# The short convolution's projections: two outputs by seven block products on x scaled by r, and the second projection in one piece in a written-out order

## The chip, the cores and the metric

The kernel runs on one core of one Trainium2 chip. The metric is the device time of one execution in microseconds; the time of a kernel is the median over its runs. All data are fp32.

## The reference

The kernel computes a trunk of two layers on 1024 tokens of width 1024. Every sub-layer works on a normed input and adds its result to x. The first layer's token mixer is a gated short convolution, and it is the part that is changed:

```
h = rmsnorm(x) * gain            # x (1, 1024, 1024)
b, c, xv = split(h @ w_in, 3)    # w_in (1024, 3072)
u = b * xv
y = causal depthwise convolution of u, width 3
x = x + (c * y) @ w_out          # w_out (1024, 1024)
x = x + swiglu(rmsnorm(x))       # hidden width 2816
```

The second layer has attention in a window of 128 in place of the convolution, and a SwiGLU of its own.

## The kernel before

**Products.** Activations lie transposed, with channels on partitions and the 1024 tokens along the free axis, as eight tiles X0 to X7. TensorE multiplies fp32 data as a rounded part hi (fp32r) and the rest lo; a product is hi*hi + hi*lo + lo*hi. `product_step` (L155, L159) does this for one block of 128 input channels: six matmuls of 128x512, three for each half of the tokens. One output tile of 128 channels takes eight steps, 48 matmuls, in two PSUM banks. Weights come by SP's queue into WR; `Weights.split` makes hi (WH, L127, or L129 on DVE) and lo (WL, L130) on the engines that it is given: in the first loop ACT and POOL, later ACT and DVE.

**Norm.** The projection multiplies x times gain, without r, the token's 1/rms. `finish_x` (L197 to L208) makes hi and lo of x times gain in XS0 to XS7 and adds up the squares. `token_r_rows` (L238) then gets r, the same on all partitions, with four 128x512 matmuls by a matrix of ones (L250, L251) in P2 and P3. As r was left out, the outputs b and xv are multiplied by its row afterwards (`times`, L173), and y once more for c.

**The projection's order.** `conv_layer` first goes over the eight input blocks as x lands, with three output tiles at once: b0, x0 and c0. Then for j = 1 to 7 it does the tiles b_j, x_j and c_j. In between, DVE and ACT make u = b*x, the taps of the convolution (L358, L360), y*r (L363), and z_j = c*y as hi and lo. After x_1 and c_1, all eight output tiles of w_out get the part of z0 and z1 (`w_out_part`), 12 matmuls for each half; the part of z2 to z7 comes at the beginning of `channel_mixer`, 18 for each half. The order of this stage is what the program order and the free buffers make it. In four of the eight turns DVE also makes sums of the mixer's first weights (`weight_sums`, L436 to L439), placed behind a given operation, which go to HBM as `first_sums`.

**The written-out order.** `channel_mixer` has an order of its own, the class `Line`. `work` appends matmuls at the line's end, at `MM` = 0.2265 us for each; `at(t, f)` puts any other step at the line time t; `run` then issues all steps so that whatever is due goes ahead of the matmuls that begin later. The line times are a plan; on the chip the engines run by their queues and semaphores. A weight's split is due `LEAD` = 13 us ahead of its first matmul and its load 7 us ahead of that.

**Seven block products.** In the mixer two output tiles of 128 channels are computed together as a 2x2 block product over pairs of input blocks and the two halves of the tokens, with seven block products for eight (the scheme of Strassen in Winograd's form). A block product (`unit_product`, `ring_granule`, `granule_work`, L544 to L547) is 12 matmuls of 128x512 on operands B[0] to B[6], which are sums and differences of blocks of x, and on weights of which four of seven are sums. The first four pairs (GROUP) run kind by kind, with sums that lie in HBM; the later ones are steady, pair by pair, with sums that DVE makes beside them. `put` makes hi (L475, ACT) and lo (L476, DVE) of an operand, and the split of a granule does the same for weights, in eight slots named G. The results are combined in `sa` and `s3`.

**The end of the convolution.** `tail_item` (L622 to L641) does one output tile of the second projection for one half of the tokens, adds it to X, and squares it; `half_chain` (L670 to L682) then makes r for that half by four 128x1 matmuls and four transposes, which leave the rows of r in a PSUM bank, and L692 scales x by the gain and those rows in place.

Of the kernel before, what the change touches and what calls it, by code (L numbers as in the profile page):

```python
# [3 lines left out]

# [5 lines left out]
F32 = mybir.dt.float32  # L10
# [4 lines left out]
P = 128  # L15
# [53 lines left out]
SUMS = {2: 0, 3: 1, 5: 2, 6: 3}  # L69
# [11 lines left out]
def trunk_kernel(ctx: ExitStack, tc: tile.TileContext, xT, small, w_in, w_out, w_qk, w_v, w_o, w_gu, w_dn, out):  # L81
# [21 lines left out]
    class Weights:  # L103
# [84 lines left out]
    def finish_x(stage, m, first, hi_eng=act, ss_eng=pool, parts=1):  # L188
# [13 lines left out]
        if first:  # L202
            state["ss"] = slot("G1")
            act.activation(state["ss"], X[m], AF.Square)
        else:
            sq = slot(("G2", "G9")[m % 2])
            act.activation(sq, X[m], AF.Square)
            ss_eng.tensor_tensor(state["ss"], state["ss"], sq, ALU.add)  # L208
# [67 lines left out]
    def conv_layer():  # L276
        groups = [[0, 1], [2, 3, 4, 5, 6, 7]]
        z = {}

        def w_out_part(g, m):  # L280
            js = groups[g]
            run(residual_tile(w_out[m][:, js[0] : js[-1] + 1, :], [z[j] for j in js], m))

        def in_tile(m, tags=("acc", "acc")):
            ps = Acc(tags)
            run(product(ps, load_w(w_in[m], NK), xs))
            return ps
# [3 lines left out]
        wb, wx, wc = Weights(), Weights(), Weights(("G6", "G7", "G8"))  # L291

        def load_b(k, n):
            wb.load(w_in[0][:, k : k + n, :], k, n)

        def load_parts(k, n):
            load_b(k, n)
            wx.load(w_in[2 * NK][:, k : k + n, :], k, n)
            wc.load(w_in[NK][:, k : k + n, :], k, n)
# [15 lines left out]
        wx.load(w_in[2 * NK][:, 0:1, :], 0, 1)  # L315
        wc.load(w_in[NK][:, 0:1, :], 0, 1)
        load_x(1)
        load_parts(1, 1)
        for k in range(NK):
# [12 lines left out]
            run(product_step(ps_b, wb, state["xs"][k], k, k == 0, k == NK - 1))  # L332
            run(product_step(ps_x, wx, state["xs"][k], k, k == 0, k == NK - 1))
            run(product_step(ps_c, wc, state["xs"][k], k, k == 0, k == NK - 1))
        xs = [state["xs"][k] for k in range(NK)]
        b0 = slot("G10")
        for src, c in ps_b.parts:
            act.copy(b0[:, c], src)
        rb = token_r_rows()

        for j in range(NK):
            t1 = slot(f"G{3 + j % 2}")
            if j > 0:
                ps_b = in_tile(j)
                times(t1, ps_b, rb)
            else:
                dve.tensor_tensor(t1, b0, rb, ALU.mult)
            if j == 2:
                for m in range(NK):
                    w_out_part(0, m)  # L350
            if j > 0:
                ps_x = in_tile(2 * NK + j)
            u = slot(f"G{5 + j % 2}")
            times(u, ps_x, rb)
            dve.tensor_tensor(u, u, t1, ALU.mult)
            y = slot(f"G{7 + j % 2}")
            cw = [cst[:, C_CONV + w * NK + j : C_CONV + w * NK + j + 1] for w in range(NCONV)]
            act.activation(y, u, AF.Copy, scale=cw[2])  # L358
            for s in (1, 2):
                dve.scalar_tensor_tensor(  # L360
                    y[:, s:T], u[:, 0 : T - s], cw[2 - s], y[:, s:T], ALU.mult, ALU.add
                )
            y_op = dve.tensor_tensor(y, y, rb, ALU.mult)  # L363
            if j > 0:
                ps_c = in_tile(NK + j)
            if 3 <= j < 7:
                n = j - 3
                for i in (0, 1):
                    weight_sums(first_sums[0][n], w_gu[0, n], w_gu[0, NF + n], 2 * i, 2, f"G{9 + i}", "G11", behind=y_op)
            z[j] = pair_slot(f"A{j % 6}")  # L370
            for c in [slice(0, T)] if j + 1 < NK else [lo_half, hi_half]:
                for src, cc in ps_c.parts:
                    if c.start <= cc.start < c.stop:
                        dve.tensor_tensor(y[:, cc], src, y[:, cc], ALU.mult)
                act.copy(z[j][:, 0, c], y[:, c])
                dve.tensor_tensor(z[j][:, 1, c], y[:, c], plain(z[j][:, 0, c]), ALU.subtract)
        js = groups[1]
# [64 lines left out]
    def weight_sums(dst, w1, w2, j0, n, raw_tag, sum_tag, line=None, t=0.0, behind=None):  # L442
# [10 lines left out]
        def add():  # L453
            raw = it["raw"]
            s = it["s"] = slot(sum_tag, (P, 4, 2 * P), bufs=2 if sum_tag == "WL" else 1)[:, :, 0 : n * P]
            for f in sums_of(raw[:, 0, 0], raw[:, 0, 1], raw[:, 1, 0], raw[:, 1, 1], s[:, 0], s[:, 1], s[:, 2], s[:, 3]):
                op = f()
                if behind is not None:
                    issue_behind(op, behind, "of use to the mixer only")
# [13 lines left out]
    def split_steps(out_hi, out_lo, raw):  # L473
# [1254 lines left out]
```

## Time and profile before

| | |
|---|---|
| median of 3 runs | 1975.11 us (1974.98 to 1975.17) |
| profiled execution | 1974.93 us |
| its span | 1973.1 us |
| PE, matmuls | 99% of the span busy |
| PEld, weight loads | 83% |
| DVE / ACT / POOL | 67% / 41% / 14% |
| TensorE clock granted | 1.0 of full speed |
| transfers | 293.96 MB, mean 149 GB/s |

Times are microseconds unless marked ns. PE is TensorE's matmuls and PEld its weight loads, which overlap them; DVE is VectorE, ACT ScalarE, POOL GpSimd, SP SyncE, whose queue issues most loads. A line of the order of time has the start, the duration, the engine, the source line, the operation, output<-inputs by the program's names, partitions x elements, and a count; in brackets stands the idle time before it and who ended it. A line of the waits has who waited for whom, the total, the number of times and the longest. A line of the windows has the length, then busy time and instructions of PE, PEld, DVE, ACT and POOL, the granted clock, the DMA engines' busy share and GB/s. A line of the transfers has output<-input, the issuing queue, the count, the size of one and its median time to landing.

### The profile page before, as it was taken

To read this page: it belongs to the slowest core of one execution; us is meant where nothing else is said; L and a number is where in the kernel's file an instruction comes from. 1 tells how busy PE (TensorE), PEld (TensorE's weight loads), DVE (VectorE), ACT (ScalarE), POOL (GpSimd) and SP (SyncE) were. 2 spreads that over 40 slices of the span, in tenths; PEclk is the share of its full clock that TensorE was granted. 3 is DMA by queue.
4 is the path that set the end of the run, shared out by engine and by line. 5 is a ranking of instruction groups with operands and counts; after the bars stand their busy time and mean duration, and the time that the engine had idled before them with its cause. 6 is when DMAs were issued, how large, how long until landed. Compare 5 with 4: busy or idle time off the path is not lost.

```text
span 1973.1 us, 25617 instructions
## 1 busy us (share of the span) xinstructions
PE 1963.0 (99%) x9253; PEld 1637.8 (83%) x9253; DVE 1323.0 (67%) x2367; ACT 808.6 (41%) x1557; POOL 270.9 (14%) x399
## 2 busy tenths in 40 slices
PE   9999999999999999999999999999999999999999
PEld 7888888888888888888898888888888888888887
DVE  7545457767767667765745888888677777675543
ACT  5111125533333334444524777645333333344441
POOL 4000001001111111000003445410011111110000
PEclk9999999999999999999999999999999999999999
DMA  5123325245555546986410000051455554478563
GB/s 176 33 75 113 111 92 186 77 148 186 188 174 184 190 149 238 336 289 204 130 52 22 22 7 17 28 185 58 158 176 182 197 190 164 148 264 278 202 225 104
DMA packets 139214, 293.96 MB, mean 149 GB/s; under 512 B 13520, under 2 KB 56528, under 8 KB 139088
## 3 DMA queue, kind: packets, MB, share of 16 engines
q1 hardware_dynamic: 116064, 212.08, 32.2%
q0 software_dynamic: 22880, 80.23, 11.1%
q8 instruction: 73, 1.20, 0.2%
q14 instruction: 53, 0.43, 0.1%
q10 hardware_dynamic: 144, 0.03, 0.0%
HBM read 207.87 MB, written 84.41 MB: 148 GB/s over the span
## 4 chain that ended last, share of the span: by engine, by line
PE 95%; DVE 3%; ACT 1%; DMA 1%; issue 1%; ACTq 0%; DVEq 0%
PE acc L155 14%; PE acc L544 13%; PE acc L547 13%; PE acc L545 13%; PE P L547 8%; PE P L544 8%; PE P L545 8%; PE acc L159 7%; PE acc L624 1%; PE acc L622 1%; PE acc L623 1%; PE P L1363 1%; PE P L1311 1%; PE P L1100 1%; PE P L1188 1%; PE P L1312 1%
## 5 line engine op out<-in xcount | busy, mean ns | idle before, releaser
L155 PE MATMUL acc<-XS,WH 128*128 128x512 f32 x1152 | 325.5, 395 | 0.8 <-ACT WH L127 0.6
L544 PE MATMUL acc<-XS,G 128*128 128x512 f32 x774 | 301.6, 390 | 0.0
L547 PE MATMUL acc<-XS,G 128*128 128x512 f32 x774 | 301.2, 389 | 0.0
L545 PE MATMUL acc<-XS,G 128*128 128x512 f32 x774 | 301.1, 389 | 0.0
L155 PEld LDWEIGHTS acc<-XS,WH 128*128 128x128 f32 x1152 | 207.6, 188 | 37.2 <-ACT WH L127 0.7
L159 PE MATMUL acc<-XS,WL 128*128 128x512 f32 x576 | 178.2, 391 | 0.0
L547 PEld LDWEIGHTS acc<-XS,G 128*128 128x128 f32 x774 | 145.3, 188 | 30.2
L545 PEld LDWEIGHTS acc<-XS,G 128*128 128x128 f32 x774 | 145.3, 188 | 30.1
L544 PEld LDWEIGHTS acc<-XS,G 128*128 128x128 f32 x774 | 145.3, 188 | 30.0
L544 PE MATMUL P<-A,G 128*128 128x512 f32 x422 | 164.2, 389 | 0.0
L545 PE MATMUL P<-A,G 128*128 128x512 f32 x422 | 164.2, 389 | 0.0
L547 PE MATMUL P<-A,G 128*128 128x512 f32 x422 | 164.2, 389 | 0.0
L547 PE MATMUL acc<-A,G 128*128 128x512 f32 x370 | 143.9, 389 | 0.0
L544 PE MATMUL acc<-A,G 128*128 128x512 f32 x370 | 143.9, 389 | 0.0
L545 PE MATMUL acc<-A,G 128*128 128x512 f32 x370 | 143.9, 389 | 0.0
L475 ACT CAST G<-WR 128x512 fp32r<-128x512 f32 (+1 forms) x172 | 103.6, 603 | 63.2 <-PE acc L547 31.1
L476 DVE TENSOR_TENSOR G<-WL,G 128x512 fp32r<-128x512 f32 x144 | 98.6, 686 | 45.7 <-ACT G L475 45.7
L791 ACT ACTIVATE G<-G 128x512 f32<-128x512 f32 x88 | 55.7, 633 | 161.9 <-DVE G L862 157.8
L476 DVE TENSOR_TENSOR G<-WR,G 128x512 fp32r<-128x512 f32 (+1 forms) x172 | 114.3, 665 | 10.7 <-ACT G L475 10.4
L127 ACT CAST WH<-WR 128x256 fp32r<-128x256 f32 (+2 forms) x81 | 46.5, 583 | 178.7 <-PE acc L155 154.7
L159 PEld LDWEIGHTS acc<-XS,WL 128*128 128x128 f32 x576 | 104.2, 188 | 18.1
L475 ACT CAST G<-WH 128x512 fp32r<-128x512 f32 (+1 forms) x136 | 81.4, 599 | 75.4 <-PE acc L547 39.5
(301 smaller groups left out, 3883.6 us busy)
## 6 DMA issues: line engine op xcount, KB each, us to landing
G<-h SPq DMA_DIRECT2D x70, 512.0 KB, 5.0
h<-X POOLq DMA_DIRECT2D x44, 512.0 KB, 5.2
X<-in_w_dn SPq DMA_DIRECT2D x80, 256.0 KB, 3.7
s<-X POOLq DMA_DIRECT2D x40, 512.0 KB, 4.8
WR<-in_w_gu SPq DMA_DIRECT2D x36, 512.0 KB, 6.2
WH<-in_w_gu SPq DMA_DIRECT2D x36, 512.0 KB, 6.7
h<-X POOLq DMA_DIRECT2D x66, 256.0 KB, 3.9
WR<-s SPq DMA_DIRECT2D x44, 256.0 KB, 3.5
```

The lines of the kernel that those rows point to most:

```text
L127: act.copy(self.hi[:, c], self.raw[:, c])
L155: pe.matmul(ps.half(h), wh, xs[:, j, c], start=first and j == 0, stop=False)
L159: pe.matmul(ps.half(h), wl, xs[:, 0, c], start=False, stop=last)
L475: lambda: act.copy(out_hi, raw),
L476: lambda: dve.tensor_tensor(out_lo, raw, plain(out_hi), ALU.subtract),
L544: pe.matmul(ps, w[:, 0, c], x[:, 0, :], start=start and e == 0, stop=False, skip_group_check=True)
L545: pe.matmul(ps, w[:, 0, c], x[:, 1, :], start=False, stop=False, skip_group_check=True)
L547: pe.matmul(ps, w[:, 1, c], x[:, 0, :], start=False, stop=last, skip_group_check=True)
L622: pe.matmul(ps, hi[:, kc], xs[:, 0, c], start=k == 0, stop=False)
L623: pe.matmul(ps, hi[:, kc], xs[:, 1, c], start=False, stop=False)
L624: pe.matmul(ps, lo[:, kc], xs[:, 0, c], start=False, stop=k == n_op - 1)
L791: state["silu"] = act.activation(x, x, AF.Silu)
```

## The change

- The rows of r are made before the projection ends, from `mean` (eight 128x1 matmuls) and `turn` (eight transposes), and stay in P2 and P3. X is scaled by gain and r in place (`scale`).
- The tiles b0, x0 and c0 are computed as before in the first loop, and c1 behind them, all from x without r. They go to HBM (`keep`), come back later (`back`) and are then multiplied by r's rows.
- The other 20 output tiles are ten pairs (`plan_`): b_j with x_j for j = 1 to 7, and c2 with c3, c4 with c5, c6 with c7. Each is done by seven block products on the scaled X. Four pairs form the group, whose weight sums POOL makes at the start, in place and by way of HBM (`sums_in_place`); six are steady.
- The last two block products of the last pair are interleaved with the first half of the first two tiles of the second projection (`lead_in`), which now takes all eight z at once, 24 matmuls for each half of a tile.
- The whole stage has the written-out order of a `Line`, which the mixer continues.
- The mixer's own first sums are made by POOL, in place, in eight pieces during the steady pairs; the lo parts of the first weights are made by DVE and no longer by POOL.
- w_in lies in HBM as pairs of blocks (`_pair_tiles`), so that the loads of the first tiles are runs of 128 floats (`load_pairs`).

`scheme` and `operands_of` are the functions of the mixer's order and its `put`, moved out so that both stages can use them.

```diff
-SUMS = {2: 0, 3: 1, 5: 2, 6: 3}
+SUMS = {2: 3, 3: 0, 5: 2, 6: 1}
...
+        def load_pairs(self, src, k0, n):
+            c = slice(k0 * P, (k0 + n) * P)
+            p = slice(k0 // 2 * P, (k0 + n + 1) // 2 * P)
+            nc.sync.dma_start(
+                self.raw[:, c].rearrange("p (k e c) -> p e k c", e=min(n, 2), c=P),
+                src[:, k0 % 2 if n == 1 else 0 : k0 % 2 + 1 if n == 1 else 2, p].rearrange("p e (k c) -> p e k c", c=P),
...
-        groups = [[0, 1], [2, 3, 4, 5, 6, 7]]
...
+        xs = {}
...
-        wb, wx, wc = Weights(), Weights(), Weights(("G6", "G7", "G8"))
+        wb, wx, wc = Weights(), Weights(), Weights(("G8", "G6", "G7"))
+        wc1 = Weights(("G9", "G10", "G8"))
...
-                wb.split(k, n, act, pool)
-                wx.split(k, n, act, pool)
-                wc.split(k, n, act, pool)
+                for w in (wb, wx, wc):
+                    w.split(k, n, act, dve)
...
+            if k < NK - 2:
+                for ps, w in ((ps_b, wb), (ps_x, wx), (ps_c, wc)):
+                    run(product_step(ps, w, state["xs"][k], k, k == 0, False))
...
-        rb = token_r_rows()
-        for j in range(NK):
...
+            wc1.split(k, 2, act, dve)
...
+        line = Line()
+        at = line.at
+        line.end = -2 * 18 * MM
+        for k in (NK - 2, NK - 1):
+            for ps, w in ((ps_b, wb), (ps_x, wx), (ps_c, wc)):
+                line.work(6, run, product_step(ps, w, xs[k], k, False, k == NK - 1))
...
+        def mean():
+            ps = bank("P3")
+            for b in range(NB):
+                pe.matmul(ps[:, b : b + 1], state["ss"][:, b * P : (b + 1) * P], ones, start=True, stop=True)
+            r["m"] = slot("rs_m", (P, NB))
+            r["r"] = slot("r", (P, NB))
+            dve.tensor_scalar(r["m"], ps[:, 0:NB], 1.0 / D, EPS, ALU.mult, ALU.add)
+            rsqrt(r["r"], r["m"], (P, NB))
+        def turn():
+            for h in (0, 1):
+                rows[h] = bank(("P2", "P3")[h])
+                for b in range(4):
+                    row = r["r"][:, 4 * h + b : 4 * h + b + 1]
+                    pe.transpose(rows[h][:, b * P : (b + 1) * P], row.to_broadcast([P, P]), ident)
+        at(-7.6, mean)
+        at(-5.0, turn)
+        tools = scheme(line, ["G0", "G3", "G6", "G7", "G1", "G2", "G4", "G5"])
...
+        plan_ = [("bx", 1), ("bx", 2), ("bx", 3), ("cc", 2), ("bx", 4), ("bx", 5), ("cc", 4), ("bx", 6), ("bx", 7), ("cc", 6)]
...
+        in_sums = [tc.dram_tile((4, P, 4 * P), F32, name=f"s0_{u}") for u in range(GROUP)]
+        for u in range(GROUP):
+            sums_in_place(line, in_sums[u], *sources(u), 0, 4, f"A{2 + u}", -30.0 + u, -19.0 + u)
...
+        def scale(h, m):
+            c = halves[h]
+            g = cst[:, C_GAIN + m : C_GAIN + m + 1]
+            dve.scalar_tensor_tensor(X[m][:, c], X[m][:, c], g, rows[h], ALU.mult, ALU.mult)
...
+        keep("b0", ps_b, "G4", -2.6)
+        keep("x0", ps_x, "G5", -1.3)
+        keep("c0", ps_c, "G11", 0.1)
+        for p in range(4):
+            t = -3.2 + 1.4 * p
+            at(t, scale, 0, 2 * p)
+            put(0, p, part(p, 0, 0), t + 0.7)
...
+            t = 60.0 + 2.6 * p
+            at(t, t_sum, part(p, 1, 0), part(p, 1, 0), t2(p))
+            put(4, p, part(p, 1, 0), t + 0.7)
+        ps_c1 = Acc()
+        c1 = product(ps_c1, wc1, xs)
+        for _ in range(3 * NK):
+            line.work(2, next, c1)
+        keep("c1", ps_c1, "G9", line.end + 0.05)
...
+        sa_tags = ["G11", "G10", "G8", "G9", "G11", "G8", "G9", "G8", "G9", "G8"]
...
+        def taps(j, h, u_of, t):
+            w = [cst[:, C_CONV + i * NK + j : C_CONV + i * NK + j + 1] for i in range(NCONV)]
+            c = halves[h]
+            def first():
+                if h == 0:
+                    Y[j] = slot(f"X{j}")
+                act.activation(Y[j][:, c], u_of()[:, c], AF.Copy, scale=w[2])
+            def add(s):
+                a = max(c.start, s)
+                y = Y[j][:, a : c.stop]
+                dve.scalar_tensor_tensor(y, u_of()[:, a - s : c.stop - s], w[2 - s], y, ALU.mult, ALU.add)
+            at(t, first)
+            at(t + 0.8, add, 1)
+            at(t + 0.85, add, 2)
...
+        def unit_product(u, k, tag, direct):
+            kind, j = plan_[u]
+            name = {0: "a", 1: "b1", 2: "a", 3: "a", 4: "a", 5: "b", 6: "b" if direct else "b6"}[k]
+            get = bank_at(u, name, tag)
+            start = k in (0, 1, 5) or k == 6 and not direct
+            ops_of = lambda: B[k]
+            w1, w2 = sources(u)
+            if not direct:
+                src = {0: w1[:, 0], 1: w1[:, 1], 4: w2[:, 1]}
+                src = src[k] if k in src else in_sums[u][SUMS[k]]
+                ring_granule(4, ops_of, 0, get, start, True, src=src)
...
+                if direct:
+                    at(t + 0.05, lambda: act.copy(sa(1), get()))
...
+        for k in (0, 1, 6, 5, 2, 3, 4):
+            for u in range(GROUP):
+                unit_product(u, k, "acc" if k in (0, 2, 3, 4) else f"P{u % 2}", False)
+        group_end = line.end
...
+        steady(GROUP, 0)
+        steady(GROUP, 1)
+        for u in range(GROUP, n_units):
+            unit_weights(u, line.end)
+            if u + 1 == n_units:
+                break
+            for k in (2, 5, 3):
+                steady(u, k)
+            steady(u + 1, 0)
+            steady(u, 4)
+            steady(u, 6)
+            steady(u + 1, 1)
...
+        t = group_end
+        last = line.end
+        for i in range(2 * GROUP):
+            u = i // 2
+            t_i = t + 17.4 + 8.6 * i
+            sums_in_place(
+                line, first_sums[0][u], w_gu[0, u], w_gu[0, NF + u], 2 * (i % 2), 2, ("X7", "G10")[i % 2], t_i, t_i + 7.0
+            )
+        back("c1", "G11", t + 27.0)
+        at(t + 37.0, gate_back, 1, "c1")
+        back("c0", "G11", t + 39.0)
+        back("b0", "G10", t + 8.0)
+        back("x0", "X0", t + 8.5)
+        at(t + 18.0, lambda: dve.tensor_tensor(R["b0"], R["b0"], R["x0"], ALU.mult))
+        taps(0, 0, lambda: R["b0"], t + 19.5)
+        taps(0, 1, lambda: R["b0"], t + 21.5)
+        at(t + 49.0, gate_back, 0, "c0")
...
+        def lead_in(part):
+            u = n_units - 1
+            s = line.end
+            for k in (2, 5, 3):
+                steady(u, k)
+            part(0, 0, range(4))
+            steady(u, 4)
+            part(0, 1, range(4))
+            steady(u, 6)
...
+            return {(0, 0): 4, (0, 1): 4}
...
         channel_mixer(
             0,
             2,
-            lambda m: w_out[m][:, js[0] : js[-1] + 1, :],
-            [z[j] for j in js],
-            raw_tags=("XS4", "XS5"),
+            lambda m: w_out[m],
+            z,
+            raw_tags=("XS0", "XS1"),
+            s2_tag="XS2",
             extra_tags=("XS6", "XS7"),
             keep_tags=None,
+            line=line,
+            lead_in=lead_in,
             slots=(
                 ("XS0", "XS1"),
...
+    def sums_in_place(line, dst, w1, w2, j0, n, tag, t_load, t):
+        c = slice(j0 * P, (j0 + n) * P)
+        it = {}
+        def load():
+            raw = it["raw"] = slot(tag, (P, 2, 2, n * P))
+            for i, w in enumerate((w1, w2)):
+                nc.sync.dma_start(raw[:, i], w[:, :, c])
+        def add():
+            raw = it["raw"]
+            a11, a12, a21, a22 = raw[:, 0, 0], raw[:, 0, 1], raw[:, 1, 0], raw[:, 1, 1]
+            pool.tensor_tensor(a11, a11, a21, ALU.subtract)
+            pool.tensor_tensor(a21, a21, a22, ALU.add)
+            pool.tensor_tensor(a22, a22, a11, ALU.subtract)
+            pool.tensor_tensor(a12, a12, a22, ALU.subtract)
+            nc.gpsimd.dma_start(dst[:, :, c].rearrange("s p c -> p s c"), raw.rearrange("p w e c -> p (w e) c"))
+        line.at(t_load, load)
+        line.at(t, add)
...
-        def tail_item(h, m):
+        tails = {}
+        def tail_part(h, m, ks):
             c = slice(h * HALF, h * HALF + HALF)
+            if (h, m) not in tails:
+                tails[h, m] = tail_weights(h, m, line.end), bank_at(("tail", h, m), "x", "acc")
+            w, get = tails[h, m]
+            for k in ks:
...
+        def tail_item(h, m, k0=0):
+            c = slice(h * HALF, h * HALF + HALF)
+            tail_part(h, m, range(k0, n_op))
...
+        first_items = {}
+        if lead_in is not None:
+            first_items = lead_in(tail_part)
+        origin = line.end - sum(first_items.values()) * 3 * MM
+        begin1 = origin + 8 * tail
+        begin2 = origin + 16 * tail
         for h in (0, 1):
             for m in range(NK):
-                tail_item(h, m)
+                tail_item(h, m, first_items.get((h, m), 0))
...
-        "w_in": _tiles(inp["conv_w_in"][0]),
+        "w_in": _pair_tiles(inp["conv_w_in"][0]),
```

More of the change, by code (lines that the diff above doesn't have):

```diff
@@ new lines, in conv_layer, with back, mult @@
+        steady = lambda u, k: unit_product(u, k, {1: "P1", 5: "P0", 6: "P0"}.get(k, "acc"), True)
+        steady(GROUP, 0)
[10 more added lines that the diff above has]
+            steady(u + 1, 1)
+        R = {}
+        def back(name, tag, t):
+            def load():
+                R[name] = slot(tag)
+                nc.sync.dma_start(R[name], kept[name])
+            def mult(h):
+                dve.tensor_tensor(R[name][:, halves[h]], R[name][:, halves[h]], rows[h], ALU.mult)
+            at(t, load)
+            for h in (0, 1):
+                at(t + 8.0 + 0.7 * h, mult, h)
@@ L455, in add @@
             s = it["s"] = slot(sum_tag, (P, 4, 2 * P), bufs=2 if sum_tag == "WL" else 1)[:, :, 0 : n * P]
[L456 to L459, printed above, removed]
+            for f in sums_of(raw[:, 0, 0], raw[:, 0, 1], raw[:, 1, 0], raw[:, 1, 1], s[:, 3], s[:, 0], s[:, 2], s[:, 1]):
+                f()
         def store():
@@ L508, in rooms @@
             return out_
-        ring = deque([f"G{(3 + i) % RING}" for i in range(RING)])
+        ring = deque(ring_tags)
         def ring_room():
```

349 lines of the change are left out of this document (252 added, 97 removed).

## The prediction

> **What bounds the kernel now.** I read the page first, then who TensorE (PE) waits for, then PE's own order of time.
>
> ```profile
> span 1973.1 us, 25617 instructions
> PE 1963.0 (99%) x9253; PEld 1637.8 (83%) x9253; DVE 1323.0 (67%) x2367; ACT 808.6 (41%) x1557; POOL 270.9 (14%) x399
> PEclk9999999999999999999999999999999999999999
> ...
> PE P L1311 <- DVE mx L1333: 1.8, 4, 0.6
> PE P L311 <- DVE s L308: 1.5, 1, 1.5
> ...
> PE acc L624 <- DVE A L476: 0.2, 1, 0.2
> ```
>
> The reader is to see that PE is busy in the whole span, at full granted clock, and that the list of its waits is short: these are its first, second and last of eight rows, none longer in total than 1.8 us, and most of them lie in the attention layer. So the time is the number of matmuls times their pitch, and a change pays what it takes off PE as long as nothing else arrives late. The pitch stands in PE's order of time:
>
> ```profile
> 10.43 1.07 PE L155 MATMUL acc<-XS,WH 128*128 128x512 f32 x4
> 11.79 1.07 PE L155 MATMUL acc<-XS,WH 128*128 128x512 f32 x4
> ...
> 39.36 0.39 PE L250 MATMUL P<-G,s 128*128 128x512 f32 x1
> ...
> 40.27 1.07 PE L155 MATMUL acc<-XS,WH 128*128 128x512 f32 x4
> ...
> 361.81 0.95 PE L670 MATMUL P<-cst,s 128*128 128x1 f32 x8
> 362.62 0.49 PE L544 MATMUL acc<-XS,G 128*128 128x512 f32 x1
> 362.94 0.40 PE L545 MATMUL acc<-XS,G 128*128 128x512 f32 x1
> ...
> 364.80 0.60 PE L682 MATMUL P<-cst,hr_t 128*128 128x128 f32 x4
> 365.15 0.48 PE L544 MATMUL acc<-XS,G 128*128 128x512 f32 x1
> 365.47 0.40 PE L545 MATMUL acc<-XS,G 128*128 128x512 f32 x1
> ```
>
> One product step is six matmuls 512 wide, and the next begins 11.79 - 10.43 = 1.36 us later: 0.2267 us each. The four matmuls of token_r_rows (L250, L251) take 40.27 - 39.36 = 0.91 us, the same pitch. Four 128x1 sums of squares (half_chain, L670) take 362.62 - 361.81 = 0.81 us, and the matmul behind them starts its follower 0.32 us later and not 0.227: 0.09 us more. Four transposes (L682) take 0.35 us and the same 0.09.
>
> **What PE loses and gains.** Before, the first projection is 24 tiles of 48 matmuls; after, 4 tiles (b0, x0, c0, c1) stay at 48 and 20 become 10 pairs of 7 block products of 12: 192 + 840 = 1032 for 1152, 120 less. token_r_rows goes, 4 less. The second projection stays at 384 (before 8 x 12 + 16 x 18, after 16 x 24). mean adds 8 sums, turn adds 8 transposes. The order of the built programs agrees: 7957 matmuls 512 wide before, 7833 after. So: -124 x 0.2267 = -28.1 us; sums 2 x 0.81 + 0.09 = +1.7; transposes 2 x 0.35 + 0.09 = +0.8. Together -25.6 us. This part has no cover to lose, because PE is the path. If the sums and transposes were free, it would be -28.1.
>
> **The start.** The lo parts of the first weights move from POOL to DVE (15 subtractions); the weights come as runs of 128 floats and no longer 256; four more loads (c1's weights) and eight of 512 KB (the pairs whose sums are made first) join SP's queue behind x.
>
> ```profile
> 18.33 0.30 PEld L159 LDWEIGHTS P<-XS,G 128*128 128x128 f32 x2 [0.45 <-POOL G L130]
> ...
> 26.02 1.75 DVE L208 TENSOR_TENSOR G<-G,G 128x1024 f32<-128x1024 f32 x1
> ...
> 29.38 1.21 DVE L208 TENSOR_TENSOR G<-G,G 128x1024 f32<-128x1024 f32 x1
> ...
> 21.60 1.73 POOL L130 TENSOR_TENSOR G<-G,G 128x256 fp32r<-128x256 f32 x1
> ...
> 1051.41 0.73 POOL L130 TENSOR_TENSOR WL<-WR,WH 128x256 fp32r<-128x256 f32 x1 [36.53 <-ACT WH L127]
> ...
> WR<-in_w_in SPq DMA_DIRECT2D x6, 128.0 KB, 5.7
> ...
> WR<-in_w_in SPq DMA_DIRECT2D x4, 64.0 KB, 4.2
> ...
> L1500 POOL TENSOR_TENSOR XS<-A,XS 128x512 fp32r<-128x512 f32 x4 | 5.1, 1289 | 0.0
> ...
> 18.00:20.00 2.00, 1.97 (x9) 1.39 (x8) 2.00 (x2) 2.00 (x3) 2.00 (x3) 1.00 1.04 379
> ...
> 22.00:24.00 2.00, 2.00 (x11) 1.65 (x10) 2.00 (x2) 2.00 (x4) 2.00 (x2) 1.00 0.00 0
> ```
>
> A DVE subtraction of 1024 takes 1.75 us beside POOL's and 1.21 when POOL has stopped; POOL's 256 take 1.73 beside DVE's and 0.73 alone (last columns of the windows: DMA share, GB/s). Without POOL, DVE gains 0.5 us on each of about a dozen such operations and pays about 15 x 0.35 us for the splits, estimated as parts of the 1.21. So DVE ends its start near 30 to 31 us as before, and PE's wait of 0.45 us for POOL goes. In step 0 one split comes ahead of x's second half on DVE, which I price at 0.15 us. The shorter runs can delay the weights of steps 2 and 3. No row shows their price. The nearest are the loads of 64 KB, which are runs of 128 floats already, in 4.2 us, and those of 128 KB in runs of 256 in 5.7: two of the first would be issued where one of the second was, so at one end nothing, at the other the difference of 1.5 us. I take -0.3 us in all, ends -0.45 and +1.5: the transfers stop by 22 us (the window of 22 to 24 us has 0), while the last weights are used near 31.
>
> **The rest of the projection: who could be late.** In the written order a weight's split is issued 13 us ahead of its product, so a late split costs nothing until 12 us are gone; what counts is the clearing of PSUM. I count time as the written order does, with 0 at the end of c0's product (near 39.4 us in the trace, in the changed kernel 2.5 us later).
>
> ```profile
> 457.32 0.68 DVE L476 TENSOR_TENSOR G<-WR,G 128x512 fp32r<-128x512 f32 x1
> 457.92 0.69 DVE L862 TENSOR_TENSOR G<-P,G 128x512 f32<-128x512 f32 x1
> ...
> 365.43 1.41 DVE L692 SCALAR_TENSOR_TENSOR X<-X,cst,P 128x512 f32<-128x512 f32 x2 [1.20 <-PE P L682]
> ...
> 30.62 1.14 ACT L247 CAST G<-G 128x512 fp32r<-128x512 f32 x2 [5.11 <-DVE G L208]
> ...
> 450.00:500.00 50.00, 50.00 (x222) 41.39 (x222) 39.20 (x69) 17.94 (x33) 8.10 (x12) 1.00 0.54 187
> ...
> s<-X POOLq DMA_DIRECT2D x40, 512.0 KB, 4.8
> ...
> WR<-s SPq DMA_DIRECT2D x44, 256.0 KB, 3.5
> ```
>
> DVE starts a 512-wide operation each 0.60 us (457.92 - 457.32), with a scalar each 0.67, ACT a cast each 0.55. From 0 to the first tile of the second projection PE needs 207 + 2.5 = 209 us. DVE has 270 instructions there: 217 x 0.60 + 48 x 0.67 + 5 x 1.2 = 168 us, 80%. The mixer's stage from 450 to 500 us runs the same scheme with DVE busy 39.2 of 50 us (78%), and PE is busy 50.00 there. That is the nearest row for the whole stage, and it says that this load fits.
>
> The new sums on POOL disturb that: 16 operations of 512 (1.29 us alone) for the first four pairs and 32 of 256 (0.73) for the mixer's sums, 44 us alone. Beside DVE they last 1.73/0.73 = 2.4 times as long: 104 us, in which DVE works at 1.21/1.75 = 0.69. DVE loses 0.31 x 104 = 32 us at most: 200 of 209 us. It still fits, as a mean. The Trainium skill, page "SBUF — State Buffer", section "Who interferes with whom", says that a DVE instruction with two SBUF inputs and a GpSimd instruction that reads SBUF exclude each other, the second blocking until the first ends. The rows agree that they collide; 1.21 + 0.73 = 1.94 us for a pair by that rule, where the trace has 1.75, so they overlap a little. By the rule DVE would lose 44 us, 212 of 209, and the time would be 3 us longer.
>
> Two places are tighter than the mean. **First, the sums of the first four pairs**, which PE multiplies from line time 32.6 on. Their first load lands near 24.5 us (1.6 MB behind the x that is in at 20, at 379 GB/s). POOL then makes two sums beside a busy DVE (3.1 us each), four while DVE is almost empty (31 to 36 us), and ten beside a DVE that spends half of its time on pairs in SBUF ((1.29 + 3.1)/2 = 2.2 us): done at 58 us, line time 16 to 19. The store of 1 MB is at most two of the 4.8 us row, the load back 3.5 us: line time 29 to 32. The load's cast is due at 27.8, and SP's next loads, ACT's casts and on DVE the clearing of P0 (due 30.0, needed at 32.6) queue behind it. So it just fits; I take 0. **Second, the turn into the steady pairs**, line times 95 to 118: sums for two pairs, the gates of tiles 2 and 3, b0 x x0 coming back and its taps give DVE 41 instructions, about 27 us of work in 23 us. Followed by hand from the same pitches, x4's product of half 1 ends on DVE near 115; ACT's tap waits for it, and behind that tap stand a cast and the copy out of `acc` that the next block product (due at 116.9) needs: that copy ends at 116.6. Slack 0.3 us, before POOL's first sum for the mixer (four operations at 1.73 us from 111.4: 0.31 x 6.9 = 2.1 us off DVE). I take +0.5 us, ends 0 and +2. Any wait of PE sets DVE right again, as both follow one order.
>
> The handover into the second projection I cost at nothing. Its tiles are 24 matmuls long (5.4 us) and not 18, so each split of 1024 has more cover than before; the first tile's z parts are due 5 us ahead; the third tile's cast waits 1.3 us for WH to come free and still ends 0.5 us ahead. If that cover were gone, it would be about 1 us, once.
>
> Sum: -25.6 - 0.3 + 0.5 = -25.4 us. The profiled execution took 1974.93 us, 1.8 us around its span and 0.18 us under the median of 1975.11. 1974.93 - 25.4 = 1949.5, and as a median 1949.7.
>
> **The rivals.**
> - DVE falls behind at several places and the gain shrinks by 3 to 10 us: 1953 to 1960. For it: the 0.3 us of slack at 116.9, and POOL's eight later pieces, each with 2.1 us off DVE. Against: after line time 145 DVE has a quarter of its time free. By the skill's rule above it would be 1953.
> - POOL's first sums come late. If all of the last ten run at 3.1 us, they end at line time 27, the fourth pair's sums are back near 40, and P0 is cleared at 42, not 32.6: 9.5 us, 1959. It decides as soon as POOL ends after line time 18.
> - Slower than before: DVE becomes the bound of the whole projection. If its instructions kept the start's pitch throughout (1.75/1.21 = 1.45 times), 168 would be 244 us for 209: 35 us, 1985. It decides at (209 + 25)/270 = 0.87 us for an instruction of DVE. For it: every split waits for ACT, and ACT for DVE's products, so idle time adds to work. Against: POOL contends in at most half of the stage, and the mixer's row above.
> - A gain nearly whole (PE at -28 us) would need sums and transposes that cost nothing: 1947.
>
> **How the numbers follow.** The forecast case, waits up to 3 us in all, gets 0.62 and 1948 to 1953; the first rival 0.17; the second 0.08; slower 0.08; near no change 0.02; the last 0.03. The range 1947.9 to 1959 takes the forecast with the ends of its start, most of the first rival and the second, 0.85 in all. About 0.2% (4 us) is what a measurement here can tell from nothing: faster 0.90, same 0.02, slower 0.08.
>
> **What would show it.** In the changed profile PE's busy share stays at 99%; the matmuls on XS and WH fall, those of the granules rise; PE's list of waits shows under 3 us more than before; its first product of granules starts 10.9 us after c0's end; POOL's last 512-wide sum ends before 60 us. I am wrong if PE waits for DVE or ACT for more than 5 us between 40 and 250 us, if PE idles near 72 us behind P0 or a G tile whose source is the first sums, or if the granted clock falls below 1.0.

## The result, and the profile after

The changed kernel took 1985.53 us (median of 5 runs, 1981.29 to 1986.38) where the kernel before took 1975.11: a ratio of 1.0046 with a 95% interval of 1.0031 to 1.0061. It is slower by about 10 us, and the forecast was 1949.7. The profiled span went from 1973.1 to 1983.8 us. All medians leave out one disturbed execution, of three_edits below, which took 11228.51 us.

The head of the page of the changed kernel:

```profile
span 1983.8 us, 25807 instructions
PE 1966.8 (99%) x9153; PEld 1621.8 (82%) x9153; DVE 1393.3 (70%) x2488; ACT 859.9 (43%) x1678; POOL 310.7 (16%) x436
```

The first rows of its list of TensorE's waits (who waited, for whom, us in total, times, longest):

```profile
PE P L366 <- DVE r L227: 2.8, 1, 2.8
PE P L902 <- DVE G L520: 2.5, 1, 2.5
PE P L902 <- DVE s L526: 2.4, 1, 2.4
```

PE is busy 99% of the span, as before, and has 100 matmuls fewer, but its busy time is longer. Three new waits stand in the list, 7.7 us in all, all for DVE in the changed stage. That explains a smaller gain, not a loss. The rest shows even in a stretch that the change doesn't touch, the second layer's mixer. Below is the same window of 100 us of both kernels, first before, then after (length, then busy time and number of instructions on PE, PEld, DVE, ACT, POOL; granted clock; DMA).

```profile
1500.00:1600.00 100.00, 100.00 (x443) 82.81 (x442) 73.51 (x130) 34.99 (x64) 14.74 (x22) 1.00 0.53 185
```

```profile
1500.00:1600.00 100.00, 100.00 (x434) 81.32 (x433) 71.21 (x126) 32.68 (x60) 13.98 (x21) 1.00 0.52 179
```

PE is busy without a break in both, at full granted clock, and nothing waits, but 434 matmuls go through where 443 did: 2% fewer. The same matmuls have another pitch. Over all recorded starts that lie 215 to 262 ns apart, the excess over 226.67 ns adds up to 2.9 us before and 28.3 us after. So the 10.7 us of span come out like this: PE's own work -25.6 us (the sum of the forecast), the pitch +25.5, the three waits +7.7, and two stretches of 3.41 us in which the clock stood at half speed behind two of these waits (below), +3.4; that is +11.0. The 0.3 us by which it is too much were not taken apart; the start is in them.

The pitch changes sharply from one block product to the next. These are rows of PE's order of time in the changed kernel, each the first matmul of a block product of 12:

```profile
56.69 0.39 PE L902 MATMUL acc<-A,G 128*128 128x512 f32 x1
...
59.42 0.39 PE L902 MATMUL acc<-A,G 128*128 128x512 f32 x1
...
62.14 0.40 PE L902 MATMUL acc<-A,G 128*128 128x512 f32 x1
...
64.93 0.39 PE L902 MATMUL acc<-A,G 128*128 128x512 f32 x1
...
67.73 0.39 PE L902 MATMUL P<-A,G 128*128 128x512 f32 x1
...
109.39 0.39 PE L902 MATMUL acc<-XS,G 128*128 128x512 f32 x1
...
112.12 0.39 PE L902 MATMUL acc<-XS,G 128*128 128x512 f32 x1
...
114.84 0.39 PE L902 MATMUL acc<-XS,G 128*128 128x512 f32 x1
...
117.56 0.39 PE L902 MATMUL acc<-XS,G 128*128 128x512 f32 x1
...
120.28 0.40 PE L902 MATMUL acc<-XS,G 128*128 128x512 f32 x1
...
123.08 0.39 PE L902 MATMUL acc<-XS,G 128*128 128x512 f32 x1
...
125.87 0.39 PE L902 MATMUL acc<-XS,G 128*128 128x512 f32 x1
...
128.66 0.40 PE L902 MATMUL acc<-XS,G 128*128 128x512 f32 x1
...
131.44 0.39 PE L902 MATMUL acc<-XS,G 128*128 128x512 f32 x1
```

From 109.39 on, with operands in XS tiles, there are four products of 2.72 or 2.73 us (12 x 0.2267) and four of 2.78 to 2.80 (12 x 0.2325). A period of eight is the ring of eight weight slots, whose order in this stage is G0, G3, G6, G7, G1, G2, G4, G5: the slow four are G4, G5, G0, G3. In the built program these four, with A0, A1 and s0, begin at 192 modulo 256 bytes in each partition; all other large tiles begin at 64. `mean` is the cause: at that point of the program it asks for the small tiles `rs_m`, `r` and `rs_t` for the first time, 128 B in all, and what is placed behind them is shifted by 128 B. In the kernel before these tiles came last, and every large tile lies at 64. The first four rows turn the test round: their operands are A0 and A1 (192), and there G0 and G3 (192) take 2.73 and 2.72 us, while G6 and G7 (64) take 2.79 and 2.80. So it is not an address that is slow, but the difference between the address of the weights and that of the streamed operand. With every recorded start of the changed kernel laid beside the addresses of the built program, 2975 starts with weights and operand 128 B apart average 232.7 ns, and 4018 with both alike 228.4 (226.9 for all in the kernel before). About 7 of the 28 us so lie on pairs that are alike; why they are not at 226.9 as well is open.

### The profile page after: what moved, and what is told of

The parts are those of the page before. It is cut to its first block, busy times and chain, and to the rows that moved or that the text cites. A ratio compares the mean times of both kernels' runs of the same rounds, so it can differ in the third digit from the quotient of the medians.

```text
span 1983.8 us, 25807 instructions
## 1 busy us (share of the span) xinstructions
PE 1966.8 (99%) x9153; PEld 1621.8 (82%) x9153; DVE 1393.3 (70%) x2488; ACT 859.9 (43%) x1678; POOL 310.7 (16%) x436
## 4 chain that ended last, share of the span: by engine, by line
PE 91%; DVE 5%; ACT 1%; issue 1%; DMA 1%; SPq 0%; DVEq 0%; ACTq 0%
PE acc L902 15%; PE acc L905 15%; PE acc L903 15%; PE P L902 9%; PE P L905 9%; PE P L903 9%; PE acc L165 5%; PE acc L169 2%; PE acc L1032 2%; PE acc L1030 2%; PE acc L1031 2%; PE P L1766 1%; PE P L1591 1%; PE P L1714 1%; PE P L1503 1%
## 5 line engine op out<-in xcount | busy, mean ns | idle before, releaser
L902 PE MATMUL acc<-XS,G 128*128 128x512 f32 x894 | 352.0, 394 | 0.0
L905 PE MATMUL acc<-XS,G 128*128 128x512 f32 x894 | 351.2, 393 | 0.0
L903 PE MATMUL acc<-XS,G 128*128 128x512 f32 x894 | 350.9, 393 | 0.0
L902 PE MATMUL P<-A,G 128*128 128x512 f32 x502 | 197.5, 393 | 2.5 <-DVE G L520 2.5
L905 PEld LDWEIGHTS acc<-XS,G 128*128 128x128 f32 x894 | 168.1, 188 | 38.4
L903 PEld LDWEIGHTS acc<-XS,G 128*128 128x128 f32 x894 | 168.3, 188 | 37.8
L902 PEld LDWEIGHTS acc<-XS,G 128*128 128x128 f32 x894 | 168.0, 188 | 37.7
L905 PE MATMUL P<-A,G 128*128 128x512 f32 x502 | 197.2, 393 | 0.0
L903 PE MATMUL P<-A,G 128*128 128x512 f32 x502 | 196.8, 392 | 0.0
L905 PE MATMUL acc<-A,G 128*128 128x512 f32 x410 | 161.1, 393 | 0.0
L902 PE MATMUL acc<-A,G 128*128 128x512 f32 x410 | 161.1, 393 | 0.0
L903 PE MATMUL acc<-A,G 128*128 128x512 f32 x410 | 160.6, 392 | 0.0
L842 DVE TENSOR_TENSOR G<-WL,G 128x512 fp32r<-128x512 f32 x168 | 116.8, 696 | 52.5 <-ACT G L841 52.5
L841 ACT CAST G<-WR 128x512 fp32r<-128x512 f32 (+1 forms) x198 | 119.7, 605 | 65.5 <-PE acc L905 31.8
L165 PE MATMUL acc<-XS,WH 128*128 128x512 f32 x480 | 147.5, 408 | 0.3 <-ACT WH L137 0.3
L842 DVE TENSOR_TENSOR G<-WR,G 128x512 fp32r<-128x512 f32 (+1 forms) x198 | 134.8, 681 | 12.7 <-ACT G L841 11.8
L841 ACT CAST G<-WL 128x512 fp32r<-128x512 f32 x168 | 103.5, 616 | 47.2 <-DVE WL L783 38.3
L902 PE MATMUL P<-XS,G 128*128 128x512 f32 x290 | 115.1, 397 | 2.4 <-DVE s L526 2.4
L905 PE MATMUL P<-XS,G 128*128 128x512 f32 x290 | 114.3, 394 | 0.0
L903 PE MATMUL P<-XS,G 128*128 128x512 f32 x290 | 114.3, 394 | 0.0
```

Of the source, the lines that this page charges most:

```text
L165: pe.matmul(ps.half(h), wh, xs[:, j, c], start=first and j == 0, stop=False)
L841: lambda: act.copy(out_hi, raw),
L842: lambda: lo_eng.tensor_tensor(out_lo, raw, plain(out_hi), ALU.subtract),
L902: pe.matmul(ps, w[:, 0, c], x[:, 0, :], start=start and e == 0, stop=False, skip_group_check=True)
L903: pe.matmul(ps, w[:, 0, c], x[:, 1, :], start=False, stop=False, skip_group_check=True)
L905: pe.matmul(ps, w[:, 1, c], x[:, 0, :], start=False, stop=last, skip_group_check=True)
```

## The experiments

Theory 1 is that difference. The rival, theory 2, is that the pitch is a state in which PE is left by its waits or by the halved clock. Each time is a median; the ratio is to the kernel before.

**small_first**: the small tiles ahead of the large ones, nothing else.

```diff
     cst = slot("cst", (P, C_END))
 ...
+    for tag, bufs in (("rs_m", 1), ("r", 1), ("rs_t", 2)):
+        slot(tag, (P, NB), bufs=bufs)
     X = [slot(f"X{k}") for k in range(NK)]
```

> The changed kernel with one difference: the three small tiles rs_m, r and rs_t (128 B for a partition in all) are placed ahead of the large tiles and no longer between them, so that all large tiles lie at the same address modulo 1024 (192) as each other. Instructions and their order are the same. Theory 1 (addresses: a matmul whose weights and whose streamed operand lie 128 B apart modulo 512 starts its follower about 6 ns later): the matmuls fall back to a pitch of 226.7 ns in both mixers, which takes away the 25.8 us by which the recorded starts of the changed kernel exceed that pitch; the three waits of TensorE (7.7 us) and the two halvings of its clock (3.4 us) stay: 1959.7 us, between 1957 and 1962. Theory 2 (the pitch is a state in which TensorE is left by its waits and the halved clock): nothing changes, 1981 to 1986 us.

Measured: 1959.94 us (1957.33 to 1960.95), 0.9923 [0.9908, 0.9938]. Theory 2 falls: waits of the same kind (7.0 us in all) and one halving of the clock are still there, and the pitch is back. The excess over 226.67 ns is 2.9 us, and the window of the second mixer reads as in the kernel before:

```profile
1500.00:1600.00 100.00, 100.00 (x443) 82.81 (x442) 72.09 (x128) 33.92 (x62) 13.36 (x20) 1.00 0.53 179
```

**before_128, before_256, before_64, before_32**: the kernel before with small tiles placed ahead of s0, G3, G4, G5, G0, A0 to A5 and G11, in front of `rb = token_r_rows()`. The edit is shown for 128 B; 256 B are `hr_m` and `hr_t`, 64 B `rs_m` and `r`, 32 B `r` alone.

```diff
+        for tag, shape, bufs in (("rs_m", (P, NB), 1), ("r", (P, NB), 1), ("rs_t", (P, NB), 2)):
+            slot(tag, shape, bufs=bufs)
         rb = token_r_rows()
```

> The kernel before with one difference: the same three small tiles, 128 B, are placed between the large ones (ahead of G3, G4, G5, G0 and A0 to A5), at the place where the changed kernel has them. Theory 1: half of the granules of both mixers meet weights and operands 128 B apart, as in the changed kernel (25.8 us on 7143 matmuls there, 3.6 ns each): some 6400 granule matmuls give about +23 us, 1998 us, between 1990 and 2004; the clock stays at 1.0. Theory 2: as before, 1975.1 us, since no wait and no clock changes.

> The kernel before with 256 B of small tiles (hr_m, hr_t) at that place. Theory 1 leaves the period open: if only the address modulo 256 counts, the time stays at 1975.1 us; if more of it counts, it is slower by 10 to 25 us. Theory 2: 1975.1 us.

> The kernel before with 64 B of small tiles (rs_m, r) at that place. Theory 1: if the banks are 64 B or finer in this respect, slower by 10 to 25 us as with 128 B; if the address counts in units of 128 B, 1975.1 us. Theory 2: 1975.1 us.

> The kernel before with 32 B (r alone) between the large tiles at the place of before_64 (1995.7), before_128 (1998.5) and before_256 (1975.0). If any difference in the address modulo 256 counts: slower by 15 to 25 us, 1990 to 2000. If it counts in units of 64 B: 1975.

Measured: 128 B 1998.48 us (1.0120 [1.0105, 1.0135]); 256 B 1975.01 (1.0002 [0.9992, 1.0011]); 64 B 1995.73 (1.0106 [1.0089, 1.0123]); 32 B 2001.00 (1.0132 [1.0117, 1.0148]). No instruction differs between these four and the kernel before, and the granted clock is 1.0 in all. The second mixer's window, first with 128 B, then with 256 B:

```profile
1500.00:1600.00 100.00, 100.00 (x435) 81.44 (x434) 71.00 (x126) 32.75 (x61) 12.61 (x19) 1.00 0.49 169
```

```profile
1500.00:1600.00 100.00, 100.00 (x443) 82.81 (x442) 73.64 (x130) 34.98 (x64) 14.78 (x22) 1.00 0.54 185
```

A shift of 32, 64 or 128 B costs 21 to 26 us, one of 256 B nothing: of the shifts tried, only what is left modulo 256 counts. What in the chip does this was not tried.

The next runs go after the waits that are left, in small_first:

```profile
PE P L904 <- DVE G L522: 3.3, 1, 3.3
PE P L904 <- DVE s L528: 2.6, 1, 2.6
...
PE P L368 <- DVE r L229: 1.1, 1, 1.1
```

**r_early**: c1's splits behind the chain of r.

```diff
-        for k in range(0, NK, 2):
-            wc1.split(k, 2, act, dve)
 ...
         at(-5.0, turn)
+        for i in range(4):
+            at(-6.8 + 0.9 * i, wc1.split, 2 * i, 2, act, dve)
```

> small_first with one edit: the splits of c1's weights (four casts on ACT, four subtractions of 256 on DVE) are no longer issued ahead of the chain that makes r, but behind it, one each 0.9 us of line time from -6.8 on. Theory A (the wait of TensorE for r is DVE's queue: the chain's five small operations stand behind those four subtractions, 1.36 us each beside POOL): the wait for r (1.09 us in the profile of small_first) goes, and the time is 1 us less, or 2.8 where the clock also dips in the run: 1957 to 1959. Rival B (the chain itself, ACT's two steps between DVE's, is too long for its place): the wait stays at 1 us or more and the time at 1960.

Measured: 1960.10 us, 0.9920 [0.9904, 0.9937]. The wait for r was 0.5 us and not 1.1, and the time did not move. That does not bear out theory A. In the profile of small_first the four subtractions were over by 30.4 us, and DVE stood idle for 3.88 us ahead of the chain; the wait came from the chain's last operation, which took 2.07 us beside POOL's sums (0.17 in lo_later):

```profile
34.23 0.17 DVE L360 TENSOR_SCALAR rs_m<-P 128x8 f32<-128x8 f32 x1 [3.88 <-PE P L357]
...
36.04 2.07 DVE L229 TENSOR_TENSOR r<-r,rs_t 128x8 f32<-128x8 f32 x1
```

Nor is this wait the same from one execution to the next: up to r, the programs of small_first, lo_later, pool_moved and operand_moved are one, and their profiles have 1.1, 0, 1.7 and 0 us of it. With r_early's edit, three_edits has 1.4. The subtractions that were put back came out later in DVE's queue, from 37.31 to 42.01 us, and the wait for the clearing became longer:

```profile
PE P L904 <- DVE G L522: 4.1, 1, 4.1
PE P L904 <- DVE s L528: 2.4, 1, 2.4
...
PE acc L904 <- ACT G L411: 0.8, 1, 0.8
```

**lo_later**: the lo part of an operand 1.3 us behind its hi, for the projection alone (`lag` stays 0.9 in the mixers).

```diff
-            line.at(t + 0.9, lambda: it["steps"][1]())
+            line.at(t + lag, lambda: it["steps"][1]())
```

> small_first with one edit: the lo part of each operand of the projection is issued 1.3 us behind its hi and no longer 0.9, so that in DVE's queue the scaling of the next block, where the spacing allows it, stands ahead of the subtraction that waits for ACT's cast. Theory A (the wait of 3.3 us for P's clearing near 74 us is DVE standing idle 0.4 to 0.9 us at each such subtraction, eight times): the wait falls under 1 us and the time by about 3: 1957. Rival B (DVE has too many instructions there, idle or not): the wait stays above 2.5 us and the time at 1960.

Measured: 1956.14 us (1955.10 to 1957.04), 0.9900 [0.9886, 0.9915]: 3.8 us gained. The time is the one that theory A gives, but the wait for the clearing fell only from 3.3 to 2.1 us; the one for r is gone from the list by no work of this edit (see r_early). DVE was idle 2.5 us between 40 and 80 us in place of 6.8. So idle time in DVE's queue was a part of the cause; the other is work, since DVE's 47 instructions in these 40 us took 0.80 us of busy time each (43 and 0.77 in small_first), not 0.60 to 0.67, with POOL's first sums beside them in the first half.

**pool_later**: five of POOL's eight pieces of the mixer's sums behind the projection.

```diff
-            t_i = t + 17.4 + 8.6 * i
+            t_i = t + (17.4 + 8.6 * i if i < 3 else (105.0, 110.5, 121.5, 126.5, 131.5)[i - 3])
 ...
-... ("X7", "G10")[i % 2], t_i, t_i + 7.0
+... ("X7", "G10", "X7", "G9", "XS3", "G8", "G9", "XS3")[i], t_i, t_i + 7.0
```

> small_first with one edit: of the eight pieces of the mixer's first sums on POOL, the last five are made behind the projection (line time 199 to 226, in G9, XS3 and G8) and no longer during its last three pairs. Theory A (the wait of 2.6 us near 194 us comes from DVE's operations taking 1.1 to 1.2 us beside POOL for 0.69): the wait falls under 1 us, and with it the dip of the clock behind it: 3 to 4 us less, 1956. Rival B (DVE is full there without POOL): the wait stays at 2 us or more.

Measured: 1961.13 us (1958.88 to 1963.41), 0.9926 [0.9910, 0.9941]. The wait of 2.6 us near 194 us is gone, so DVE was indeed slowed by POOL there, but the time did not improve. New waits stand in the second projection, in the profile of the fastest execution:

```profile
PE acc L1034 <- DVE WL L844: 2.7, 3, 1.6
...
PE acc L1032 <- ACT WH L843: 1.5, 1, 1.5
```

The weights of w_out come late: in SP's queue their loads stand behind loads of x, w_gu and POOL's pieces that wait for their tiles, and one row of that queue is 7.37 us long:

```profile
241.68 7.37 SPq L305 DMA_DIRECT2D X<-in_xT  x2
249.11 0.90 SPq L121 DMA_DIRECT2D WR<-in_w_out  x2
```

**three_edits**: r_early, lo_later and pool_later together.

> small_first with the three edits together. Theory A for all three: no wait of TensorE above 1 us between 30 and 250 us, clock 1.0, pitch 226.7 ns: the sum of the forecast without its waits, 1949 to 1951 us. If one of the waits is of another kind, it stays, with 1 to 3 us each and 1.7 us for a dip of the clock: 1953 to 1957.

Measured: 1957.17 us (1957.16 to 1958.09), 0.9907 [0.9891, 0.9924]. The expectation of theory A, 1949 to 1951, is missed by over 6 us: pool_later's waits in the second projection stay (2.3 and 0.9 us), with 1.9 us for the clearing and 1.4 for r.

**pool_moved**: lo_later, and POOL's five pieces earlier than in pool_later, in tiles that are free.

```diff
+            t_i = t + (17.4 + 8.6 * i if i < 3 else 62.0 + 8.0 * (i - 3))
 ...
+... ("X7", "G10", "X7", "G11", "G10", "G11", "G10", "G11")[i], t_i, t_i + 7.0
```

> lo_later with one more edit: of POOL's eight pieces the first three stay, the last five are made between line times 156 and 188 (before: 137 to 172), in G11 and G10, so that none runs beside DVE between 128 and 156, where TensorE waited 2.5 us near 191 us, and all are stored before the second projection. Theory A (that wait is DVE beside POOL, and what pool_later lost came from pieces too late for SP's queue in the second projection): the wait goes, the dip of the clock with it, no waits after 250 us: 3 to 4 us under lo_later's 1956.1, 1952 to 1953. Rival B (DVE is full there, and POOL's pieces only move the wait): a wait of 2 us stays somewhere between 190 and 250 us, 1955 to 1957.

Measured: 1952.84 us (1950.93 to 1953.57), 0.9887 [0.9872, 0.9902]: the best version, 22.0 us faster than the kernel before beside it and 32.7 faster than the changed one. The wait near 191 us is gone and the clock stays at 1.0. What is left in its list of the stage's waits is 3.5 us:

```profile
PE P L905 <- DVE G L523: 1.8, 1, 1.8
...
PE P L368 <- DVE r L229: 1.7, 1, 1.7
```

**operand_moved**: pool_moved with the operands B[6] 4.5 us later.

```diff
-            t = 17.0 + 1.7 * p
+            t = 21.5 + 1.7 * p
```

> pool_moved with one more edit: the operands of the third kind of block product (B[6], first read at line time 35.6) are scaled and split from line time 21.5 on and no longer from 17.0, so that fewer instructions stand ahead of the clearing of P0 (due at 24.5) in DVE's queue. Theory A (order in DVE's queue): the wait of 2.1 us near 71 us falls under 0.5, 1950 to 1951 us: the forecast's sum. Rival B (too much work in that stretch, in any order): the wait moves to B[6] or to the next clearing with about the same length, no gain against pool_moved.

Measured: 1953.69 us, 0.9895 [0.9878, 0.9911]. Rival B holds: the wait for the clearing of P became 2.3 us in two parts, and a new one of 2.0 us stands between them. In neither of the two orders tried does DVE keep up between 50 and 80 us.

```profile
PE P L905 <- DVE G L523: 2.3, 2, 1.4
PE P L905 <- ACT A L844: 2.0, 1, 2.0
```

**moved_back**: pool_moved with the three small tiles back between the large ones (the two lines of small_first taken out).

> pool_moved with the three small tiles back at the place where the changed kernel has them, so that G0, G3, G4, G5, A0 and A1 lie 128 B off the other large tiles again. Theory 1 (the cost of the addresses does not depend on the waits): 1952.8 + 25.8 = 1978.6 us, slower than the kernel before, though the order of the work is the best one found. If most of the 25 us had come with the waits and the clock: under 1970 us.

Measured: 1977.75 us (1.0012 [1.0002, 1.0021]), 24.9 us more than pool_moved. The price of the addresses is the same with other waits and no halved clock, and by itself it takes the whole gain of 22 us.

## Why the prediction was wrong

**The step that failed is the first one**: "the time is the number of matmuls times their pitch", with 0.2267 us taken as the pitch for the whole changed kernel. The count was right. The pitch was treated as a property of the matmul, and it belongs to a pair of addresses. No term of the sum and no rival held what a new small tile does to the placement of the others, although the change asks for `rs_m`, `r` and `rs_t` ahead of G4, A0, A1, G0, G5 and G3. It cost 25 to 26 us, by chance almost exactly the gain: small_first (-25.6 us, with one halving of the clock fewer) and moved_back (+24.9) show it from both sides. The trace of before could not have shown it, since all its large tiles lie alike; the addresses of the two built programs show that this changes, though not what it costs.

**The stalls were mis-sized**: "I take +0.5 us, ends 0 and +2". In the changed kernel they are 7.7 us of waits and 3.4 us of halved clock. None of the three has the cause of one of the two tight places. The first sums were in time, and the turn into the steady pairs passed without a wait. The waits came at the chain of r, which the prediction counted as eight sums and eight transposes of PE and not as a chain on DVE; at the first clearing of P0; and in the last pairs, where 512-wide operations of DVE took up to 1.25 us beside POOL's later pieces and 0.69 without. So two of its signs of being wrong came: the clock fell below 1.0, and PE idled behind P0 near 72 us, though not for the first sums. POOL's last 512-wide sum, and PE's wait:

```profile
53.50 1.62 POOL L833 TENSOR_TENSOR A<-A 128x512 f32<-128x512 f32 x1
...
75.85 0.47 PE L902 MATMUL P<-A,G 128*128 128x512 f32 x1 [2.50 <-DVE G L520]
```

The chain of r, in DVE's order of time:

```profile
30.95 5.44 DVE L140 TENSOR_TENSOR G<-G,G 128x256 fp32r<-128x256 f32 x4
36.32 0.15 DVE L358 TENSOR_SCALAR rs_m<-P 128x8 f32<-128x8 f32 x1
...
38.93 0.17 DVE L227 TENSOR_TENSOR r<-r,rs_t 128x8 f32<-128x8 f32 x1
```

PE was through with the sums of squares by 33.5 us, but in this execution c1's four subtractions held DVE to 36.39 and the chain ended at 39.10; in small_first they were done in time, and an operation of the chain itself was slow (see r_early). The subtractions that moved to DVE were priced at 0.35 us each; beside POOL, which has the new sums now, c1's, of the same size, take 1.36 (in small_first they take 0.36, and there a 512-wide sum of POOL that runs beside them takes 4.42 in place of 1.28). The other mistake was to judge DVE by a mean. The mean itself came as forecast: DVE was busy 185 of 212 us (45.81 to 258), where the prediction has 168 without POOL's sums and up to 200 with them. But in the middle of the stage, without POOL, it is at 93%, and at 97% where POOL's pieces run and the third wait stands:

```profile
80.00:100.00 20.00, 20.00 (x88) 16.04 (x87) 18.45 (x30) 11.47 (x21) 0.00 (x0) 1.00 0.36 99
100.00:120.00 20.00, 20.00 (x89) 16.40 (x88) 19.02 (x32) 10.05 (x19) 0.00 (x0) 1.00 0.39 126
120.00:140.00 20.00, 20.00 (x88) 16.29 (x88) 18.34 (x29) 6.95 (x13) 0.00 (x0) 1.00 0.16 52
...
180.00:200.00 20.00, 17.59 (x72) 14.04 (x71) 19.44 (x25) 7.19 (x14) 12.32 (x13) 0.93 0.75 254
```

The mean hid stretches in which DVE has no room left to catch up.

**What was right**: the sum for PE. `mean` took 1.70 us (31.65 to 33.35; 1.71 by the rows), `turn` 0.85 (0.79). The first block product starts 10.9 us behind c0's end (45.81 to 56.69). With the addresses alike and 3.5 us of waits, pool_moved's span is 21.3 us under that of before; without these waits it would be 24.8, where the forecast has 25.4. The rival of late DVE (1953 to 1960) describes small_first. The slower rival named 1985 us, which is what came, but that is luck, as its mechanism did not happen: DVE held PE for 7.7 us, not for 35.

## What to carry to other kernels

Before a change's cost is summed, compare the addresses that the old and the new program give to the tiles that TensorE reads; a small tile asked for in a new place shifts all that follow. Place small tiles first or last, or keep weights and streamed operands alike modulo 256 B. In a trace, count the matmuls for 100 us in a stage that was not changed: neither the busy share nor the list of waits shows a pitch that is 2% longer.

## What the runs showed of the hardware

- A 128x512 matmul of the block products starts its follower after 226.7 ns where weights and streamed operand are alike modulo 256 B, and after about 232.5 where they differ by 128 B (2.72 and 2.79 us for 12); a shift of 32 or 64 B costs the whole kernel as much (before_32, before_64). The Trainium skill, page "TensorE: Matmul & The Clock Gate", section "Step-by-step: what each phase is for", says that loading the next weights takes no read bandwidth of SBUF from the running matmul, as the two have a read port each. The runs do not fit this: by the rule the addresses of both together would not matter, and before_128 would have had the time of before_256. What happens between the two reads is not shown.
- Half speed came in windows of 3.41 us on one fixed grid: the two of the changed kernel begin 157.0 us apart, which is 46 such windows. Windows of the changed kernel around its three waits, each pair being the window with most of the wait and the next one:

```profile
36.80:40.20 3.40, 1.05 (x9) 1.05 (x10) 2.36 (x5) 0.16 (x1) 3.24 (x3) 1.00 0.38 141
40.20:43.60 3.40, 3.40 (x10) 2.61 (x9) 1.05 (x2) 1.28 (x3) 2.88 (x4) 0.50 0.47 183
70.90:74.30 3.40, 2.45 (x11) 1.69 (x9) 3.31 (x6) 2.17 (x5) 0.00 (x0) 1.00 0.28 67
74.30:77.80 3.50, 1.95 (x9) 1.62 (x10) 3.38 (x7) 0.63 (x3) 0.00 (x0) 1.00 0.43 112
193.80:197.20 3.40, 1.22 (x6) 0.64 (x4) 3.40 (x4) 3.16 (x6) 2.92 (x3) 1.00 0.55 154
197.20:200.60 3.40, 3.17 (x8) 2.50 (x9) 3.17 (x6) 0.01 (x1) 2.07 (x3) 0.50 0.79 307
```

The waits of 2.8 and 2.4 us fell into one window each, which left PE 1.05 and 1.22 us of busy time in 3.4, and the next window ran at half speed. The wait of 2.5 us was split between two windows (2.45 and 1.95 us busy) and cost nothing more. The same page of the Trainium skill, section "What's actually happening", has a free-running window of 3413 ns, and the trace agrees; that a wait of 2.4 us is enough is what these rows add. A wait of 2.4 us can so cost 2.4 or 4.1 us, and which of them depends on where it falls. The other runs, laid on the same grid, agree: ahead of the last 20 us, a full-speed window with 0.93 to 1.27 us of PE busy time was followed by half speed in all five cases, and one with 1.55 us or more in none.
